# A prefix log-sum-exp: running sums moved from fp16 matmuls into VectorE adds and 18 fp32 matmuls a tile

## Chip, cores, metric

One core of a Trainium2 chip. The metric is the device time of one execution in microseconds (us). Executions whose profile shows no disturbance are called fast.

## The reference

For an input of 4 x 4096 x 4128 fp32 (batch, row, column), every output row is the log of the sum of the exponentials of all rows up to it, column by column:

```python
def reference(x):                      # x: (4, 4096, 4128) float32
    out[:, 0, :] = x[:, 0, :]
    for t in range(1, S):
        mx = np.maximum(out[:, t-1, :], x[:, t, :])
        out[:, t, :] = mx + np.log(np.exp(out[:, t-1, :] - mx) + np.exp(x[:, t, :] - mx))
```

So it is Exp, a running sum down the rows, Ln, with 270 MB in and 270 MB out.

## The kernel before

A tile has 128 partitions with R = 3 consecutive rows each (384 rows, 6.3 MB; one tile a batch has R = 2), 44 tiles in all. A tile is worked on in four chunks of 1024 columns; the last has 32 columns more, the "tail". ScalarE writes Exp as fp16 over the tile. TensorE forms all running sums in PSUM with matrices of ones and zeros: `incl` and `excl` sum over partitions, `ident` adds a partition's next row, `pick` adds the carry of the tile above. ScalarE takes Ln out of PSUM row by row. The carry is kept by VectorE as a high and a low fp16 half.

```python
# ... (Chunk, cut)
    def head(self):
        pt = self.pt = pmain.tile([P, CH], FP32, name="pt")
        for j in range(t.r):
            for s in range(0, CH, MM):
                mm(pt[:, s:s + MM], excl if j else incl, self.e(j, s, s + MM), start=j == 0)
        if not t.first:
            for s in range(0, CH, MM):
                mm(pt[:, s:s + MM], pick, carry[self.c][:, s:s + MM])
        # ... tail cut
    def stage(self, j):
        nc.scalar.activation(t.xt[:, j, c * CH:(c + 1) * CH], pt, ACT.Ln)
        if j + 1 < t.r:
            for s in range(0, CH, MM):
                mm(pt[:, s:s + MM], ident, self.e(j + 1, s, s + MM), stop=j + 2 == t.r)
            # ... tail cut
        else:
            keep(carry[c], pt)         # VectorE: high half, then low half

# order: the Exp of chunk g + 2 is issued behind the Ln of chunks g, g - 1, g - 2
for g in range(len(chunks) + R - 1):
    for d in range(R - 1, -1, -1):
        ...
            k.stage(d)
            if k.c == last and d + 1 == k.t.r:
                k.t.store()            # then the load three tiles ahead
    if g + 2 < len(chunks):
        chunks[g + 2].exp()
    if g + 1 < len(chunks):
        chunks[g + 1].head()
```

Four tile buffers lie in SBUF; loads and stores go out on one queue, each tile one transfer in and one out.

The softmax here doesn't subtract the row's maximum and nothing guards it: scores larger than these inputs give would overflow.

Of the kernel before, what the change touches and what calls it, by code (L numbers as in the profile page):

```python
# [6 lines left out]

FP32 = mybir.dt.float32
FP16 = mybir.dt.float16
ACT = mybir.ActivationFunctionType  # L10
P = 128
R = 3
CH = 1024
MM = 512
HI, LO = 96, 32


def _constants(nc, pool):


    def tri(base, name):
        t = pool.tile([P, P], FP16, name=name)
        nc.gpsimd.memset(t, 1.0)

        nc.gpsimd.affine_select(  # L25
            out=t, in_=t, pattern=[[1, P]], compare_op=mybir.AluOpType.is_ge,
            fill=0.0, base=base, channel_multiplier=-1,
        )
        return t

    def ones_where_zero(bases, step, name):
        t = pool.tile([P, P], FP16, name=name)
        nc.gpsimd.memset(t, 0.0)
        for base in bases:
            nc.gpsimd.affine_select(  # L35
                out=t, in_=t, pattern=[[step, P]], compare_op=mybir.AluOpType.not_equal,
                fill=1.0, base=base, channel_multiplier=1,
            )
        return t

    return (
        tri(0, "incl"),
        tri(-1, "excl"),
        ones_where_zero([0], -1, "ident"),
        ones_where_zero([-(HI + 31), -(LO + 31)], 0, "pick"),
    )


@with_exitstack
def kernel(  # L50
    ctx: ExitStack,
    tc: tile.TileContext,
    x: bass.AP,
    out: bass.AP,
):






    nc = tc.nc
    B, S, D = x.shape
    assert S % P == 0
    n_main = D // CH
    tail = D - n_main * CH
    t0 = n_main * CH
    last = n_main - 1

    nc.scalar.preload_act_table_set("natural_log_exp_and_others")  # L70
    consts = ctx.enter_context(tc.tile_pool(name="consts", bufs=1))
    incl, excl, ident, pick = _constants(nc, consts)

    bufs = 4
    xpool = ctx.enter_context(tc.tile_pool(name="xpool", bufs=bufs))
    cpool = ctx.enter_context(tc.tile_pool(name="cpool", bufs=1))
    pmain = ctx.enter_context(tc.tile_pool(name="pmain", bufs=3, space=bass.MemoryType.PSUM))
    ptail = ctx.enter_context(tc.tile_pool(name="ptail", bufs=2, space=bass.MemoryType.PSUM))

    carry = [cpool.tile([P, CH], FP16, name=f"carry{c}") for c in range(n_main)]  # L80
    carry_t = cpool.tile([P, tail], FP16, name="carry_t")
    for t in (*carry, carry_t):
        nc.vector.memset(t, 0.0)  # L83

    ctx.enter_context(tc.manual_schedule())

    def mm(pt, w, rhs, start=False, stop=False):
        nc.tensor.matmul(pt, lhsT=w, rhs=rhs, start=start, stop=stop, skip_group_check=True)  # L88

    def keep(cr, pt):  # L90

        nc.vector.tensor_copy(cr[HI:HI + 32, :], pt[HI:HI + 32])  # L92
        nc.vector.tensor_tensor(  # L93
            out=cr[LO:LO + 32, :], in0=pt[HI:HI + 32], in1=cr[HI:HI + 32, :],
            op=mybir.AluOpType.subtract,
        )

    class Step:


        def __init__(self, b, row, r):
            self.b, self.row, self.r = b, row, r
            self.first = row == 0

        def dram(self, t):
            rows = t[self.b, self.row:self.row + P * self.r, :]
            return rows.rearrange("(p j) d -> p j d", j=self.r)

        def load(self):
            full = xpool.tile([P, R, D], FP32, name="xt")  # L110
            self.xt = full[:, :self.r, :]
            self.half = self.xt.bitcast(FP16)
            nc.sync.dma_start(out=self.xt, in_=self.dram(x))  # L113

        def store(self):
            nc.sync.dma_start(out=self.dram(out), in_=self.xt)  # L116

    class Chunk:
        def __init__(self, step, c):
            self.t, self.c = step, c  # L120
            self.w = D - last * CH if c == last else CH

        def e(self, j, a, b):
            return self.t.half[:, j, 2 * self.c * CH + a:2 * self.c * CH + b]

        def exp(self):
            c0, w = self.c * CH, self.w
            nc.scalar.activation(  # L128
                self.t.half[:, :, 2 * c0:2 * c0 + w], self.t.xt[:, :, c0:c0 + w], ACT.Exp,
            )  # L130

        def head(self):
            t = self.t
            pt = self.pt = pmain.tile([P, CH], FP32, name="pt")
            for j in range(t.r):
                for s in range(0, CH, MM):
                    mm(pt[:, s:s + MM], excl if j else incl, self.e(j, s, s + MM), start=j == 0)
            if not t.first:
                for s in range(0, CH, MM):
                    mm(pt[:, s:s + MM], pick, carry[self.c][:, s:s + MM])  # L140
            if self.c == last:
                self.tail_head()

        def tail_head(self):


            t, r = self.t, self.t.r
            full = ptail.tile([P, R, tail], FP32, name="qt")
            qt = self.qt = full[:, :r, :]
            to = lambda v, n: v.unsqueeze(1).to_broadcast([P, n, tail])  # L150
            for i in range(r):
                e = self.e(i, CH, CH + tail)
                mm(qt[:, i:, :], incl, to(e, r - i), start=i == 0)
                if i:
                    mm(qt[:, :i, :], excl, to(e, i))
            if not t.first:
                mm(qt, pick, to(carry_t, r))

        def stage(self, j):

            t, c, pt = self.t, self.c, self.pt
            nc.scalar.activation(t.xt[:, j, c * CH:(c + 1) * CH], pt, ACT.Ln)  # L162
            if j + 1 < t.r:
                for s in range(0, CH, MM):
                    mm(pt[:, s:s + MM], ident, self.e(j + 1, s, s + MM), stop=j + 2 == t.r)
                if c == last and j == 0:
                    nc.scalar.activation(t.xt[:, :, t0:D], self.qt, ACT.Ln)  # L167
                    keep(carry_t, self.qt[:, t.r - 1, :])
            else:
                keep(carry[c], pt)  # L170

    steps = []
    for b in range(B):
        n = S // P
        parts = [R] * (n // R) + ([n % R] if n % R else [])
        if b == 0:
            parts.reverse()
        row = 0
        for r in parts:
            steps.append(Step(b, row, r))  # L180
            row += P * r
        assert row == S

    chunks = [Chunk(s, c) for s in steps for c in range(n_main)]
    ahead = bufs - 1
    for s in steps[:ahead]:
        s.load()
    stored = 0
    chunks[0].exp()
    chunks[1].exp()  # L190
    chunks[0].head()
    for g in range(len(chunks) + R - 1):
        for d in range(R - 1, -1, -1):
            if 0 <= g - d < len(chunks) and d < chunks[g - d].t.r:
                k = chunks[g - d]
                k.stage(d)
                if k.c == last and d + 1 == k.t.r:
                    k.t.store()
                    if stored + ahead < len(steps):
                        steps[stored + ahead].load()  # L200
                    stored += 1
        if g + 2 < len(chunks):
            chunks[g + 2].exp()
        if g + 1 < len(chunks):
            chunks[g + 1].head()


# [28 lines left out]
```

## Time and profile before

| | before |
|---|---|
| time, median of 3 runs (lowest to highest) | 1262.96 us (1262.78 to 1263.07) |
| bytes moved, mean rate | 541 MB, 429 GB/s |
| ScalarE, TensorE, VectorE busy | 75%, 55%, 36% |
| mean granted TensorE clock | 0.77 |

The lines that carry the argument stand in the prediction. In its busy rows each digit is the busy share of a fortieth of the span in tenths; a group line gives the code line, engine, operation and shapes, the count, then busy us and mean ns of one, then the idle time before it and what ended it; a line of waits gives the total us, the number of waits and the longest one; a line of a timeline gives start and length in us, and `x3` merges three instructions in a row. A line of a table by stretches gives the busy us of each engine, then the granted clock, the DMA share and GB/s.

### The profile page before, as it was taken

The page shows a single profiled execution, that of the slowest core. Times are in us where ns is not written, and L with a number is a line of the kernel's source. Part 1 is how long each engine was busy: PE and PEld are TensorE (multiplying, and loading weights), DVE is VectorE, ACT ScalarE, POOL GpSimd, SP SyncE. Part 2 cuts the span into 40 slices and gives each one's busy share as a digit, 9 for nine tenths or more (in the row PEclk, how much of TensorE's full clock was granted, in tenths as well). Part 3 has the DMA queues.
Part 4 walks back from the last instruction along what each step waited for, and adds up shares of the span by engine and source line. Part 5 has one row for each costly group of instructions (what it writes and reads, how often), then busy time and mean ns, then how long its engine had stood idle before and what let it go on. Part 6 is the DMA issues. An engine that isn't in the chain of part 4 may idle for free.

```text
span 1261.0 us, 6165 instructions
## 1 busy us (share of the span) xinstructions
PE 688.7 (55%) x2268; PEld 237.0 (19%) x2268; DVE 451.4 (36%) x445; ACT 947.3 (75%) x733; POOL 2.2 (0%) x13
## 2 busy tenths in 40 slices
PE   3665554555555555655346555555634755664552
PEld 1222111111121111211112211111211211221120
DVE  2443333333333333334424333333442433333344
ACT  5997777777777777778569777777966977777794
POOL 0000000000000000000000000000000000000000
PEclk9887777777677777777768777787777777778786
DMA  9999999999999999999999999999999999999998
GB/s 411 410 439 431 432 427 434 438 430 432 433 437 431 432 432 436 432 427 436 431 433 436 437 429 431 436 436 432 430 434 435 432 431 432 434 435 431 433 422 347
DMA packets 12702, 541.46 MB, mean 429 GB/s; under 512 B 1408, under 2 KB 1408, under 8 KB 1408
## 3 DMA queue, kind: packets, MB, share of 16 engines
q1 hardware_dynamic: 12672, 541.07, 99.4%
q8 instruction: 18, 0.29, 0.1%
q14 instruction: 12, 0.10, 0.0%
HBM read 270.53 MB, written 270.53 MB: 429 GB/s over the span
## 4 chain that ended last, share of the span: by engine, by line
DMA 69%; ACT 21%; PE 5%; issue 2%; DVE 1%; SPq 0%; ACTq 0%
DMA xt<-in_x_dram 67%; ACT xt L128 11%; ACT xt L162 10%; PE pt L88 5%; DMA out_dram<-xt 2%; ACT xt L167 0%; SPq L116 0%; DVE carry L92 0%; DVE carry L93 0%; ACTq L231 0%; SPq L113 0%; ACTq L128 0%; PE qt L88 0%
## 5 line engine op out<-in xcount | busy, mean ns | idle before, releaser
L128 ACT ACTIVATE xt<-xt 128x3072 f16<-128x3072 f32 (+3 forms) x176 | 478.5, 2719 | 247.9 <-DMA xt<-in_x_dram 247.8
L88 PE MATMUL pt<-xt,ident 128*128 128x512 f16 x672 | 251.3, 470 | 530.7 <-ACT xt L162 530.4
L162 ACT ACTIVATE xt<-pt 128x1024 f32<-128x1024 f32 x512 | 487.6, 1030 | 2.5 <-PE pt L88 0.7
L92 DVE CAST carry<-pt 32x1024 f16<-32x1024 f32 x176 | 216.4, 1230 | 761.0 <-ACT xt L162 760.7
L88 PE MATMUL pt<-xt,excl 128*128 128x512 f16 x672 | 247.0, 504 | 0.0
L93 DVE TENSOR_TENSOR carry<-pt,carry 32x1024 f16<-32x1024 f32 x176 | 215.9, 1227 | 6.1
L88 PEld LDWEIGHTS <-ident 128*128 128x128 f16 x672 | 70.1, 104 | 677.7 <-issue 654.0
L88 PE MATMUL pt<-xt,incl 128*128 128x512 f16 x352 | 152.0, 526 | 23.6 <-ACT xt L128 15.0
L88 PEld LDWEIGHTS <-excl 128*128 128x128 f16 x756 | 92.5, 124 | 141.0 <-issue 108.1
L88 PE MATMUL pt<-carry,pick 128*128 128x512 f16 x320 | 109.8, 429 | 0.0
L88 PEld LDWEIGHTS <-incl 128*128 128x128 f16 x480 | 45.2, 111 | 129.7 <-DVE carry L93 95.2
L88 PEld LDWEIGHTS <-pick 128*128 128x128 f16 x360 | 40.6, 113 | 57.0 <-issue 34.3
L167 ACT ACTIVATE xt<-qt 128x96 f32<-128x96 f32 (+1 forms) x44 | 10.9, 249 | 45.7 <-PE pt L88 45.7
L92 DVE CAST carry_t<-qt 32x32 f16<-32x32 f32 x44 | 8.7, 197 | 25.5 <-ACT xt L167 25.4
L88 PE MATMUL qt<-xt,incl 128*128 128x64 f16 (+2 forms) x128 | 12.3, 196 | 0.0
L88 PE MATMUL qt<-xt,excl 128*128 128x64 f16 (+1 forms) x84 | 10.6, 187 | 0.0
L93 DVE TENSOR_TENSOR carry_t<-qt,carry_t 32x32 f16<-32x32 f32 x44 | 8.5, 193 | 1.5
L88 PE MATMUL qt<-carry_t,pick 128*128 128x96 f16 (+1 forms) x40 | 8.2, 204 | 0.0
L83 DVE MEMSET carry<- 128x512 uint32 x4 | 1.9, 485 | 1.1 <-PEq L220 1.0
L70 ACT ACT_TABLE_LOAD x1 | 1.3, 1283 | 0.8 <-PEq L220 0.8
L35 POOL TENSOR_SCALAR_AFFINE_SELECT pick<-pick 128x128 f16<-128x128 f16 x2 | 0.6, 294 | 0.1
L25 POOL TENSOR_SCALAR_AFFINE_SELECT incl<-incl 128x128 f16<-128x128 f16 x1 | 0.3, 294 | 0.0
(11 smaller groups left out, 1.9 us busy)
## 6 DMA issues: line engine op xcount, KB each, us to landing
xt<-in_x_dram SPq DMA_DIRECT2D x40, 6192.0 KB, 42.2
out_dram<-xt SPq DMA_DIRECT2D x40, 6192.0 KB, 28.1
xt<-in_x_dram SPq DMA_DIRECT2D x4, 4128.0 KB, 37.3
out_dram<-xt SPq DMA_DIRECT2D x4, 4128.0 KB, 23.0
```

The lines of the kernel that those rows point to most:

```text
L25: nc.gpsimd.affine_select(out=t, in_=t, pattern=[[1, P]], compare_op=mybir.AluOpType.is_ge, fill=0.0, base=base, channel_multiplier=-1,)
L35: nc.gpsimd.affine_select(out=t, in_=t, pattern=[[step, P]], compare_op=mybir.AluOpType.not_equal, fill=1.0, base=base, channel_multiplier=1,)
L70: nc.scalar.preload_act_table_set("natural_log_exp_and_others")
L83: nc.vector.memset(t, 0.0)
L88: nc.tensor.matmul(pt, lhsT=w, rhs=rhs, start=start, stop=stop, skip_group_check=True)
L92: nc.vector.tensor_copy(cr[HI:HI + 32, :], pt[HI:HI + 32])
L93: nc.vector.tensor_tensor(out=cr[LO:LO + 32, :], in0=pt[HI:HI + 32], in1=cr[HI:HI + 32, :], op=mybir.AluOpType.subtract,)
L128: nc.scalar.activation(self.t.half[:, :, 2 * c0:2 * c0 + w], self.t.xt[:, :, c0:c0 + w], ACT.Exp,)
L162: nc.scalar.activation(t.xt[:, j, c * CH:(c + 1) * CH], pt, ACT.Ln)
L167: nc.scalar.activation(t.xt[:, :, t0:D], self.qt, ACT.Ln)
```

## The change

The intent: fp32 throughout, no halves, and far fewer instructions. Exp stays fp32 in place. VectorE adds a partition's rows to one another (`own`); one `excl` matmul on the partition's last row adds the partitions above into a PSUM tile `above` that lives through the whole kernel; VectorE adds `above` to all rows at once (`add_above`); a `pick` matmul then starts the next tile's `above` from the last row. One Ln a chunk, in place.

```diff
-    carry = [cpool.tile([P, CH], FP16, name=f"carry{c}") for c in range(n_main)]
+    above = [psum.tile([P, CH], FP32, name=f"above{c}") for c in range(n_main)]
 ...
+        def act(self, func):
+            v = self.t.xt[:, :, self.a:self.b]
+            nc.scalar.activation(v, v, func)
+        def own(self):
+            for j in range(1, self.t.r):
+                v = x[:, j, self.a:self.b]
+                add(v, x[:, j - 1, self.a:self.b], v)
         def head(self):
-            for j in range(t.r): ... incl, excl
+            for s in range(0, CH, MM):
+                mm(above[self.c][:, s:s + MM], excl, t.xt[:, t.r - 1, a + s:a + s + MM],
+                   start=t.first, stop=True)
+        def add_above(self):
+            v = t.xt[:, :, a:a + CH]
+            add(v, v, above[self.c].unsqueeze(1).to_broadcast([P, t.r, CH]))
+        def pick(self, s0=0, s1=CH):
+            if not t.final:
+                for s in range(s0, s1, MM):
+                    mm(above[self.c][:, s:s + MM], pick, t.xt[:, t.r - 1, a + s:a + s + MM],
+                       start=True)
 ... (the tail: two small matmuls, one add and one copy; cut)
+    for g, k in enumerate(chunks):
+        if g + 1 < len(chunks):
+            chunks[g + 1].own()
+            chunks[g + 1].head()
+        if g + 2 < len(chunks):
+            chunks[g + 2].act(ACT.Exp)
+        if g:
+            finish(chunks[g - 1])      # tail add, pick of the last 512 columns
+            result(chunks[g - 1])      # Ln; behind the last chunk: store, load three ahead
+        k.add_above()
+        if k.c == last:
+            k.tail_head()
+            k.pick(0, CH - MM)
+        else:
+            k.pick()
```

More of the change, by code (lines that the diff above doesn't have):

```diff
@@ L8 @@
 FP32 = mybir.dt.float32
-FP16 = mybir.dt.float16
 ACT = mybir.ActivationFunctionType
@@ L14 @@
 MM = 512
-HI, LO = 96, 32
 def _constants(nc, pool):
-    def tri(base, name):
-        t = pool.tile([P, P], FP16, name=name)
-        nc.gpsimd.memset(t, 1.0)
-        nc.gpsimd.affine_select(
-            out=t, in_=t, pattern=[[1, P]], compare_op=mybir.AluOpType.is_ge,
-            fill=0.0, base=base, channel_multiplier=-1,
-        )
-        return t
-    def ones_where_zero(bases, step, name):
-        t = pool.tile([P, P], FP16, name=name)
-        nc.gpsimd.memset(t, 0.0)
-        for base in bases:
-            nc.gpsimd.affine_select(
-                out=t, in_=t, pattern=[[step, P]], compare_op=mybir.AluOpType.not_equal,
-                fill=1.0, base=base, channel_multiplier=1,
-            )
-        return t
-    return (
-        tri(0, "incl"),
-        tri(-1, "excl"),
-        ones_where_zero([0], -1, "ident"),
-        ones_where_zero([-(HI + 31), -(LO + 31)], 0, "pick"),
-    )
+    excl = pool.tile([P, P], FP32, name="excl")
+    nc.gpsimd.memset(excl, 1.0)
+    nc.gpsimd.affine_select(
+        out=excl, in_=excl, pattern=[[1, P]], compare_op=mybir.AluOpType.is_ge,
+        fill=0.0, base=-1, channel_multiplier=-1,
+    )
+    pick = pool.tile([P, P], FP32, name="pick")
+    nc.gpsimd.memset(pick, 0.0)
+    nc.gpsimd.affine_select(
+        out=pick, in_=pick, pattern=[[0, P]], compare_op=mybir.AluOpType.not_equal,
+        fill=1.0, base=-(P - 1), channel_multiplier=1,
+    )
+    return excl, pick
 @with_exitstack
@@ L71 @@
     consts = ctx.enter_context(tc.tile_pool(name="consts", bufs=1))
-    incl, excl, ident, pick = _constants(nc, consts)
+    excl, pick = _constants(nc, consts)
     bufs = 4
@@ L76 @@
     cpool = ctx.enter_context(tc.tile_pool(name="cpool", bufs=1))
-    pmain = ctx.enter_context(tc.tile_pool(name="pmain", bufs=3, space=bass.MemoryType.PSUM))
-    ptail = ctx.enter_context(tc.tile_pool(name="ptail", bufs=2, space=bass.MemoryType.PSUM))
-    carry = [cpool.tile([P, CH], FP16, name=f"carry{c}") for c in range(n_main)]
-    carry_t = cpool.tile([P, tail], FP16, name="carry_t")
-    for t in (*carry, carry_t):
-        nc.vector.memset(t, 0.0)
+    psum = ctx.enter_context(tc.tile_pool(name="psum", bufs=1, space=bass.MemoryType.PSUM))
+    above = [psum.tile([P, CH], FP32, name=f"above{c}") for c in range(n_main)]
+    above_t = above[last][:, CH - MM:CH - MM + tail]
+    carry_t = cpool.tile([P, tail], FP32, name="carry_t")
+    nc.vector.memset(carry_t, 0.0)
     ctx.enter_context(tc.manual_schedule())
@@ L88, in mm, with add @@
         nc.tensor.matmul(pt, lhsT=w, rhs=rhs, start=start, stop=stop, skip_group_check=True)
-    def keep(cr, pt):
-        nc.vector.tensor_copy(cr[HI:HI + 32, :], pt[HI:HI + 32])
-        nc.vector.tensor_tensor(
-            out=cr[LO:LO + 32, :], in0=pt[HI:HI + 32], in1=cr[HI:HI + 32, :],
-            op=mybir.AluOpType.subtract,
-        )
+    def add(o, a, b):
+        nc.vector.tensor_tensor(out=o, in0=a, in1=b, op=mybir.AluOpType.add)
     class Step:
@@ L103, in __init__ @@
             self.first = row == 0
+            self.final = row + P * r == S
         def dram(self, t):
@@ L111, in load @@
             self.xt = full[:, :self.r, :]
-            self.half = self.xt.bitcast(FP16)
             nc.sync.dma_start(out=self.xt, in_=self.dram(x))
@@ L120, in __init__ @@
             self.t, self.c = step, c
-            self.w = D - last * CH if c == last else CH
-        def e(self, j, a, b):
-            return self.t.half[:, j, 2 * self.c * CH + a:2 * self.c * CH + b]
-        def exp(self):
-            c0, w = self.c * CH, self.w
-            nc.scalar.activation(
-                self.t.half[:, :, 2 * c0:2 * c0 + w], self.t.xt[:, :, c0:c0 + w], ACT.Exp,
-            )
-        def head(self):
+            self.a, self.b = c * CH, D if c == last else (c + 1) * CH
@@ new lines, in act @@
+        def act(self, func):
+            v = self.t.xt[:, :, self.a:self.b]
+            nc.scalar.activation(v, v, func)
+        def own(self):
+            x = self.t.xt
+            for j in range(1, self.t.r):
+                v = x[:, j, self.a:self.b]
+                add(v, x[:, j - 1, self.a:self.b], v)
+        def head(self):
+            t, a = self.t, self.a
+            for s in range(0, CH, MM):
+                mm(above[self.c][:, s:s + MM], excl, t.xt[:, t.r - 1, a + s:a + s + MM],
+                   start=t.first, stop=True)
@@ L133, in head, with tail_head @@
+        def add_above(self):
+            t, a = self.t, self.a
+            v = t.xt[:, :, a:a + CH]
+            add(v, v, above[self.c].unsqueeze(1).to_broadcast([P, t.r, CH]))
+        def pick(self, s0=0, s1=CH):
+            t, a = self.t, self.a
+            if not t.final:
+                for s in range(s0, s1, MM):
+                    mm(above[self.c][:, s:s + MM], pick, t.xt[:, t.r - 1, a + s:a + s + MM],
+                       start=True)
+        def tail_head(self):
             t = self.t
-            pt = self.pt = pmain.tile([P, CH], FP32, name="pt")
@@ L135, in head @@
-            for j in range(t.r):
-                for s in range(0, CH, MM):
-                    mm(pt[:, s:s + MM], excl if j else incl, self.e(j, s, s + MM), start=j == 0)
             if not t.first:
-                for s in range(0, CH, MM):
-                    mm(pt[:, s:s + MM], pick, carry[self.c][:, s:s + MM])
-            if self.c == last:
-                self.tail_head()
-        def tail_head(self):
-            t, r = self.t, self.t.r
-            full = ptail.tile([P, R, tail], FP32, name="qt")
-            qt = self.qt = full[:, :r, :]
-            to = lambda v, n: v.unsqueeze(1).to_broadcast([P, n, tail])
-            for i in range(r):
-                e = self.e(i, CH, CH + tail)
-                mm(qt[:, i:, :], incl, to(e, r - i), start=i == 0)
-                if i:
-                    mm(qt[:, :i, :], excl, to(e, i))
-            if not t.first:
-                mm(qt, pick, to(carry_t, r))
@@ L159, in stage @@
-        def stage(self, j):
-            t, c, pt = self.t, self.c, self.pt
-            nc.scalar.activation(t.xt[:, j, c * CH:(c + 1) * CH], pt, ACT.Ln)
-            if j + 1 < t.r:
-                for s in range(0, CH, MM):
-                    mm(pt[:, s:s + MM], ident, self.e(j + 1, s, s + MM), stop=j + 2 == t.r)
-                if c == last and j == 0:
-                    nc.scalar.activation(t.xt[:, :, t0:D], self.qt, ACT.Ln)
-                    keep(carry_t, self.qt[:, t.r - 1, :])
-            else:
-                keep(carry[c], pt)
+                mm(above_t, pick, carry_t, start=True)
@@ L172, with tail_add @@
+            mm(above_t, excl, t.xt[:, t.r - 1, t0:D], start=t.first, stop=True)
+        def tail_add(self):
+            t = self.t
+            v = t.xt[:, :, t0:D]
+            add(v, v, above_t.unsqueeze(1).to_broadcast([P, t.r, tail]))
+            if not t.final:
+                nc.vector.tensor_copy(carry_t[96:, :], t.xt[96:, t.r - 1, t0:D])
     steps = []
@@ L188, with finish, result @@
     stored = 0
-    chunks[0].exp()
-    chunks[1].exp()
-    chunks[0].head()
-    for g in range(len(chunks) + R - 1):
-        for d in range(R - 1, -1, -1):
-            if 0 <= g - d < len(chunks) and d < chunks[g - d].t.r:
-                k = chunks[g - d]
-                k.stage(d)
-                if k.c == last and d + 1 == k.t.r:
-                    k.t.store()
-                    if stored + ahead < len(steps):
-                        steps[stored + ahead].load()
-                    stored += 1
-        if g + 2 < len(chunks):
-            chunks[g + 2].exp()
-        if g + 1 < len(chunks):
-            chunks[g + 1].head()
+    def finish(k):
+        if k.c == last:
+            k.tail_add()
+            k.pick(CH - MM)
+    def result(k):
+        nonlocal stored
+        k.act(ACT.Ln)
+        if k.c == last:
+            k.t.store()
+            if stored + ahead < len(steps):
+                steps[stored + ahead].load()
+            stored += 1
+    chunks[0].act(ACT.Exp)
+    chunks[1].act(ACT.Exp)
+    chunks[0].own()
+    chunks[0].head()
+    for g, k in enumerate(chunks):
+        if g + 1 < len(chunks):
+            chunks[g + 1].own()
+            chunks[g + 1].head()
+        if g + 2 < len(chunks):
+            chunks[g + 2].act(ACT.Exp)
[3 more added lines that the diff above has]
+        k.add_above()
+        if k.c == last:
+            k.tail_head()
+            k.pick(0, CH - MM)
+        else:
+            k.pick()
+    finish(chunks[-1])
+    result(chunks[-1])
 _INS = ['x']
```

## The prediction

> **What bounds the kernel now.** I read the page from the top: busy shares, the DMA rows, the queue, and the chain.
>
> ```profile
> PE 688.7 (55%) x2268; PEld 237.0 (19%) x2268; DVE 451.4 (36%) x445; ACT 947.3 (75%) x733; POOL 2.2 (0%) x13
> DMA  9999999999999999999999999999999999999998
> q1 hardware_dynamic: 12672, 541.07, 99.4%
> DMA 69%; ACT 21%; PE 5%; issue 2%; DVE 1%; SPq 0%; ACTq 0%
> xt<-in_x_dram SPq DMA_DIRECT2D x40, 6192.0 KB, 42.2
> out_dram<-xt SPq DMA_DIRECT2D x40, 6192.0 KB, 28.1
> ```
>
> No compute engine is above 75%; the transfers fill every slice but the last. The diff leaves them as they are: x in once, out once, 541 MB. The 42.2 us of a load and 28.1 us of a store are mostly queueing: 6192 KB (6.34 MB) at the 433 GB/s of the middle slices is 14.6 us, so a load waits behind about two such transfers and a store behind one. Next, who waits for whom, and one period of ScalarE and of the issuing queue in the middle:
>
> ```profile
> ACT xt L128 <- DMA xt<-in_x_dram: 247.8, 42, 12.2
> SPq L116 <- ACT xt L162: 1178.4, 44, 30.0
> ```
> ```profile
> 539.25 2.76 ACT L128 ACTIVATE xt<-xt 128x3072 f16<-128x3072 f32 x1 [6.04 <-DMA xt<-in_x_dram]
> ...
> 568.50 2.76 ACT L128 ACTIVATE xt<-xt 128x3072 f16<-128x3072 f32 x1 [5.99 <-DMA xt<-in_x_dram]
> ```
> ```profile
> 584.34 0.34 SPq L116 DMA_DIRECT2D out_dram<-xt  x1
> 584.78 0.38 SPq L113 DMA_DIRECT2D xt<-in_x_dram  x1
> ```
>
> ScalarE, the busiest engine, stands still for a load in every step. A full step takes 568.50 - 539.25 = 29.25 us, two transfers of 14.6 us. When a load lands (568.50) the queue still holds the store and the load issued a step earlier, 29.2 us of work. The next pair is issued 15.8 us later (584.34), so **13 us of slack** is left before the DMA would run dry. So the question is not what the engines' sums are, but whether a step still fits 29.25 us and whether its store still comes less than 29 us after the next load's landing. Slack is missing only at the ends:
>
> ```profile
> 37.00 0.35 SPq L116 DMA_DIRECT2D out_dram<-xt  x1
> ```
> ```profile
> 1225.00:1230.00 5.00, 2.21 (x9) 0.69 (x8) 2.41 (x4) 4.32 (x6) 0.00 (x0) 1.00 0.76 327
> 1230.00:1235.00 5.00, 3.98 (x10) 1.28 (x10) 2.88 (x4) 5.00 (x5) 0.00 (x0) 0.66 0.48 201
> 1235.00:1240.00 5.00, 2.75 (x12) 1.02 (x12) 4.87 (x5) 4.29 (x5) 0.00 (x0) 1.00 0.78 337
> ```
>
> The first store goes out at 37.0; the three opening loads (16.9 MB, from about 2 us) end near 41, so today it comes in time. Between 1225 and 1240 the DMA share falls to 0.48: the last load is in and the second-last store is not yet issued.
>
> **The durations I price with.**
>
> ```profile
> L128 ACT ACTIVATE xt<-xt 128x3072 f16<-128x3072 f32 x120 | 332.1, 2767 | 233.1 <-DMA xt<-in_x_dram 233.1
> L162 ACT ACTIVATE xt<-pt 128x1024 f32<-128x1024 f32 x512 | 487.6, 1030 | 2.5 <-PE pt L88 0.7 <-PE qt L88 0.3
> L93 DVE TENSOR_TENSOR carry<-pt,carry 32x1024 f16<-32x1024 f32 x176 | 215.9, 1227 | 6.1
> ```
> ```profile
> 38.80 1.03 PE L88 MATMUL pt<-xt,excl 128*128 128x512 f16 x4
> 39.66 0.59 PE L88 MATMUL pt<-carry,pick 128*128 128x512 f16 x2
> ...
> 664.20 1.93 PE L88 MATMUL pt<-xt,ident 128*128 128x512 f16 x4 [2.44 <-ACT xt L162]
> 665.92 1.06 PE L88 MATMUL pt<-xt,incl 128*128 128x512 f16 x2
> ```
>
> Start to start, a 512-column fp16 matmul takes (39.66 - 38.80)/4 = 0.215 us where the clock is granted and (665.92 - 664.20)/4 = 0.43 us where it is not.
>
> **What the Trainium skill says.** "VectorE: DVE Perf Modes", on the TRN2 errata, gives an fp32 tensor_tensor add (N+151)/0.96 ns, that is 1224 ns for N = 1024; the subtract above measured 1227 ns, with PSUM as source. It agrees, though on 32 partitions. "TensorE: Matmul & The Clock Gate", Part 1, gives N/1.2 ns cold and N/2.4 + 2.5 ns warm: 427 and 216 ns, which the two spacings confirm. "FP8 and Floating Point Precision", TensorE Precision Notes, says that true fp32 takes four passes through the array; no run so far has an fp32 matmul, so this price is the least certain. "DMA: Bandwidth & Descriptors", Specifications, puts the fabric's ceiling at 435 GB/s; the page shows 429 over the span, so there is nothing to win on transfers.
>
> **The change, part by part, for a full step** (three row groups, four chunks; 40 such steps, and 4 with two row groups).
>
> *ScalarE.* Exp stays, in place in fp32: 4 x about 2.77 us. The 12 Ln of 1030 ns and one of 250 ns become 4 Ln of Exp's shape, 2.77 us, and successive ones overlap by 0.1. 8 x 2.67 + 0.2 for the wider chunk's two = 21.6 us, where it now takes 3 x 2.76 + 2.89 + 12 x 0.9 + 0.15 = 22.1. No change worth counting; busy stays near 950 us (75%).
>
> *VectorE.* The 8 carry copies and subtracts on 32 partitions go (9.8 us). In come six 1024-wide adds at 1.23 (7.4), two of 1056 at 1.26 (2.5), four 3072-wide at (3072+151)/0.96 = 3.36 us (13.4), and the tail's add and copy (0.26 + 0.20). Sum **23.8 us of 29.25**, 81%. With two row groups it is 3 x 1.23 + 1.26 + 4 x 2.29 + 0.4 = 14.5. In all 40 x 23.8 + 4 x 14.5 = 1010 us, 80%: VectorE becomes the busiest engine.
>
> *TensorE.* Some 52 fp16 matmuls become 16 of 512 columns and 2 of 32. Four passes make 4 x 0.215 = 0.86 us warm, 1.71 cold: 13.8 us or 27.3 us a step, plus under 1 us for the small ones. Even wholly cold it stays below 29.25, and a TensorE that busy should get its clock. I expect 60 to 75% busy.
>
> *Waits.* In a steady step, t = 0 at the load's landing: ScalarE does Exp, Ln (old chunk 1), Exp, Ln (2), Exp, Ln (3), then the store of the old tile goes out. VectorE: the first own sum at 2.8 to 5.2, the add for old chunk 3 to 8.6, the second own sum (its Exp is in at 8.1) to 11.1, the old tile's tail add to 11.4. ScalarE reaches the last Ln at 5 x 2.67 = 13.4, so the tail add is in time and the store goes out at **16.2 us against 15.8 now**. VectorE goes on: add to 14.8, own 17.2, add 20.6, own 23.2, add 26.6, before the next landing at 29.25. The head matmuls of a chunk run behind the 3.4 us add of the one before. Slack stays about 13 us; the middle of the kernel doesn't move.
>
> *Ends.* Start: the first store now waits for all four Ln of tile 0, three of which stand behind Exps of tile 1. That tile's first Exp starts at 27.7; from there three Exps (2.7) and three two-row Ln (1.85) give 27.7 + 8.0 + 5.6 = 41.3 us, in place of 37.0. Its first packets follow about 1.5 us after issue (an estimate from the first load: issued 0.8, moving at 2), near 42.8, while the loads end near 41: **+1.7 us** of empty DMA, never won back. End: after the last landing, three 1.8 us Exps and three 2.75 us Ln give the second-last store at 13.7 us in place of 12.9 (1220.8 to about 1233.6): **+0.8 us**. The last store comes about 25 us after the landing, still before the one ahead of it has drained (about 30), so it hides.
>
> Sum: 1262.96 + 1.7 + 0.8 = **1265.4 us**.
>
> **Rivals.** *VectorE becomes the bound.* It needs over 29.25 us a step, 23% above my sum. For it: adds with two SBUF inputs on 128 partitions are not in this trace, and 80% is high. Against: the formula met the one measured add within 0.3%. If an add cost 2 cycles an element, a step would be near 46 us and the kernel 2000 us. *TensorE becomes the bound*, through four weight loads per fp32 matmul that don't hide, at 0.10 to 0.15 us each: cold, 16 x (1.71 + 0.5) = 35 us, about 1520 us in all; warm 21 us, and nothing. Against: a TensorE that never idles should be granted its clock. *The DMA slows beside heavier SBUF traffic.* 1% would be 12 us. Against: its rate is 434 GB/s both in busy and in idle stretches of the engines. *A gain*: the DMA floor, 541 MB at 434 GB/s, is 1247 us, so 2% faster (1238) is out of reach.
>
> **Range and chances.** Transfers alone bound it from below, and the ends' terms are each good to a microsecond: 1262 to 1270 holds it 8 times in 10. Faster by over 2%: 0.01. Within 2%: 0.94. Slower: 0.05, nearly all from the TensorE and VectorE rivals.
>
> **What would show it.** Right: the queue at 99% of the span, first store near 41, steady steps of 29.2 us with stores about 16 us after a landing, ScalarE still waiting for loads, VectorE near 1010 us with 3.36 us adds, 512-column fp32 matmuls 0.86 or 1.71 us apart. Wrong: DMA digits under 9 in the middle, ScalarE waiting for VectorE or TensorE in place of loads, 3072-wide adds far over 3.4 us, fp32 matmuls over 1.8 us, or stores over 29 us after a landing.

## The result, and the profile after

| | before | changed |
|---|---|---|
| time, median of 4 runs | 1262.97 us | 1264.09 us (1263.63 to 1268.05) |
| the same on another chip | 1262.83 us (9 runs) | 1265.39 us (1265.19 to 1265.54, 5 runs) |
| VectorE busy | 451 us (36%) | 981 us (77%) |
| TensorE busy, granted clock | 689 us (55%), 0.77 | 761 us (60%), 0.87 |

The ratio of the two is 1.0016 (95% interval 0.9996 to 1.0036) in the first set and 1.002 (1.0007 to 1.0032) in the second. Ratios are the mean time of one kernel's fast runs over that of the other's of the same rounds, so not quite the ratio of the medians. By the second set the change costs a fifth of a per cent. The profiled run of the first set happened to be its longest, 1268.05 us; the one on the other chip was 1265.3. I read timelines from the first and sums from both.

The page of the changed kernel: busy shares, the DMA row, the queue and the chain.

```profile
PE 760.5 (60%) x1512; PEld 289.0 (23%) x1512; DVE 980.6 (77%) x597; ACT 923.8 (73%) x353; POOL 1.1 (0%) x8
DMA  9999999999999999999999999999999999999998
q1 hardware_dynamic: 12672, 541.07, 99.3%
DMA 67%; DVE 12%; ACT 9%; PE 8%; issue 1%; SPq 0%; ACTq 0%
```

VectorE's work has more than doubled, and the DMA row is what it was, digit for digit. The chain is still two thirds transfers. ScalarE's waits, and one full step of ScalarE and of the issuing queue in the middle:

```profile
ACT xt L106 <- DMA xt<-in_x_dram: 290.5, 42, 12.5
ACT xt L106 <- PE above L74: 33.9, 38, 4.2
```
```profile
544.47 13.38 ACT L106 ACTIVATE xt<-xt 128x3072 f32<-128x3072 f32 x5 [7.08 <-DMA xt<-in_x_dram]
558.46 8.23 ACT L106 ACTIVATE xt<-xt 128x3168 f32<-128x3168 f32 x3 [0.61 <-PE above L74]
573.72 13.38 ACT L106 ACTIVATE xt<-xt 128x3072 f32<-128x3072 f32 x5 [7.03 <-DMA xt<-in_x_dram]
```
```profile
590.57 0.34 SPq L97 DMA_DIRECT2D out_dram<-xt  x1
```

From landing to landing it is 573.72 - 544.47 = 29.25 us, the step of the kernel before to the hundredth, and ScalarE waits 7 us in each for a load. The store goes out at 590.57 - 573.72 = 16.85 us after the landing; before it was 15.84. The middle line shows why it is later than ScalarE alone would make it: ahead of a tile's last Ln ScalarE waits 0.6 us for TensorE. That Ln works in place, and a `pick` matmul is still reading the last row of the chunk.

The durations of the new work, by shape, and TensorE's pace, first in its granted clock, then in the first group behind a pause of 6.5 us:

```profile
L106 ACT ACTIVATE xt<-xt 128x3072 f32<-128x3072 f32 x240 | 645.9, 2750 | 273.0 <-DMA xt<-in_x_dram 273.0
L77 DVE TENSOR_TENSOR xt<-xt,above 128x3072 f32<-128x3072 f32 x160 | 535.7, 3348 | 1.2
L77 DVE TENSOR_TENSOR xt<-xt 128x1024 f32<-128x1024 f32 x252 | 308.1, 1222 | 248.3 <-ACT xt L106 244.0
```
```profile
26.11 1.88 PE L74 MATMUL above<-xt,pick 128*128 128x512 f32 x4
27.83 1.88 PE L74 MATMUL above<-xt,excl 128*128 128x512 f32 x4
...
579.10 3.75 PE L74 MATMUL above<-xt,excl 128*128 128x512 f32 x4 [6.51 <-DVE xt L77]
582.64 0.47 PE L74 MATMUL above<-carry_t,pick 128*128 128x32 f32 x2
```

Each fp32 matmul of the kernel leaves two matmul records, so the `x4` are two of them: (27.83 - 26.11)/2 = 0.86 us each, and (582.64 - 579.10)/2 = 1.77 us in the slow clock.

The ends: the first two stores, and the stretch behind the last load.

```profile
42.64 0.35 SPq L97 DMA_DIRECT2D out_dram<-xt  x1
...
68.38 0.34 SPq L97 DMA_DIRECT2D out_dram<-xt  x1
```
```profile
1230.00:1235.00 5.00, 4.00 (x13) 1.78 (x12) 4.46 (x5) 5.00 (x3) 0.00 (x0) 1.00 0.83 357
1235.00:1240.00 5.00, 3.50 (x9) 1.16 (x7) 5.00 (x3) 5.00 (x4) 0.00 (x0) 1.00 0.21 89
```

The first store went out at 37.0 before and goes out at 42.6 now. The table below sums, from the records of all DMA packets, the time in which the 16 engines had no packet under way (an average over the 16, in us), leaving out the first 2 us and what follows the last store's bulk. Its last column adds what packets took beyond their usual time (1.829 us for 49.5 KB, 1.222 us for 33 KB).

```
profiled run         empty, 41-46   empty, 66-72   empty, ends of batches   gap near the end   slow packets
before                   0               0                 0                     4.0               4.5
changed                  1.9             0.2               0.3                   4.9               7.7
changed, 2nd chip        2.0             0.4               0                     3.6               6.3
```

The same records show where the time is lost. Set against the kernel before by the bytes moved so far (my sum over all packets of both traces), the changed kernel on the second chip is 0.9 us behind at 44 us, 1.7 at 60, 2.7 at 90 and 4.1 at 100; from 110 to 1225 us it stays 3.3 to 4.5 behind without a trend, and its span ends 2.5 us behind. So the loss is made in the first 100 us, the middle adds nothing and the end gives some of it back. At 44 us it is 0.9 and not 1.9 us because the last opening packets of the kernel before were slow: its loads ended at 42.5 to 43.2 us, those of the changed kernel at 41.3 to 42.1.

### The profile page after: what moved, and what is told of

Read it like the earlier page. It is cut to its first block, busy times and chain, and to the rows that moved or that the text cites. A ratio compares the mean times of both kernels' runs of the same rounds, so it can differ in the third digit from the quotient of the medians.

```text
span 1266.3 us, 4623 instructions
## 1 busy us (share of the span) xinstructions
PE 760.5 (60%) x1512; PEld 289.0 (23%) x1512; DVE 980.6 (77%) x597; ACT 923.8 (73%) x353; POOL 1.1 (0%) x8
## 4 chain that ended last, share of the span: by engine, by line
DMA 67%; DVE 12%; ACT 9%; PE 8%; issue 1%; SPq 0%; ACTq 0%
DMA xt<-in_x_dram 63%; DVE xt L77 12%; ACT xt L106 9%; PE above L74 8%; DMA out_dram<-xt 5%; SPq L97 0%; ACTq L106 0%; SPq L94 0%; DVE carry_t L146 0%
## 5 line engine op out<-in xcount | busy, mean ns | idle before, releaser
L106 ACT ACTIVATE xt<-xt 128x3072 f32<-128x3072 f32 (+2 forms) x352 | 922.5, 2693 | 327.0 <-DMA xt<-in_x_dram 290.5
L74 PE MATMUL above<-xt,excl 128*128 128x512 f32 (+1 forms) x792 | 443.1, 687 | 348.7 <-DVE xt L77 339.4
L77 DVE TENSOR_TENSOR xt<-xt 128x1024 f32<-128x1024 f32 (+1 forms) x336 | 413.4, 1230 | 255.0 <-ACT xt L106 249.4
L77 DVE TENSOR_TENSOR xt<-xt,above 128x3072 f32<-128x3072 f32 (+3 forms) x220 | 582.9, 2651 | 11.7 <-PE above L74 10.3
L74 PE MATMUL above<-xt,pick 128*128 128x512 f32 x640 | 330.7, 630 | 130.0 <-DVE xt L77 130.0
L74 PEld LDWEIGHTS above<-xt,excl 128*128 128x128 f32 x792 | 162.6, 229 | 601.5 <-issue 490.5
L74 PEld LDWEIGHTS above<-xt,pick 128*128 128x128 f32 x640 | 113.6, 198 | 307.4 <-DVE xt L77 227.2
L74 PEld LDWEIGHTS above<-carry_t,pick 128*128 128x128 f32 x80 | 20.8, 271 | 51.4 <-DVE xt L77 48.2
L74 PE MATMUL above<-carry_t,pick 128*128 128x32 f32 x80 | 17.5, 308 | 10.1 <-DVE xt L77 10.1
L146 DVE COPY carry_t<-xt 32x32 f32<-32x32 f32 x40 | 7.1, 178 | 1.4
```

The costliest lines, as they stand in the source:

```text
L74: nc.tensor.matmul(pt, lhsT=w, rhs=rhs, start=start, stop=stop, skip_group_check=True)
L77: nc.vector.tensor_tensor(out=o, in0=a, in1=b, op=mybir.AluOpType.add)
L106: nc.scalar.activation(v, v, func)
L146: nc.vector.tensor_copy(carry_t[96:, :], t.xt[96:, t.r - 1, t0:D])
```

## The experiments

All were started from the changed kernel unless said otherwise. In the first four, the same chip served all.

**1. The changed kernel again.** No edit.

> The changed kernel as it is, on the chip that the three reordered ones use. The theory (transfers bound it, the reordered ends add 1.9 us of empty DMA at the first store and 0.8 us at the last): 1264 to 1266 us, 1 to 3 us over the kernel before. The rival (the 1 us seen is chance in the packets' times): the two within 0.5 us, either way round.

Measured: 1265.39 us against 1262.83 before, ratio 1.002 (1.0007 to 1.0032). The difference of 2.6 us is real and of the predicted size. In the trace, 2.4 us of empty DMA at the start are new, and the packets ran 1.8 us slower, most of it in the first 100 us; the gap near the end was 0.4 us shorter than before, not longer. That is 3.8 us, and the two spans differ by 2.5: most of the rest is idle time that the kernel before has more of, 0.6 us behind its last store, where one of the 16 engines finished after the others, and 0.3 scattered over the middle.

**2. The first tile finished early.** At the boundary behind the first tile, the Ln of a chunk go ahead of the next tile's Exp, and the tile's last add and Ln ahead of the next tile's own sums.

```diff
+    early = {n_main}
     for g, k in enumerate(chunks):
+        ends = g + 1 in early
-        if g + 1 < len(chunks):
+        if g + 1 < len(chunks) and not ends:
             chunks[g + 1].own()
             chunks[g + 1].head()
+        if (ends or g + 2 in early) and g:
+            result(chunks[g - 1])
         ... Exp of chunk g + 2; the usual finish and result unless done; add_above, pick
+        if ends:
+            finish(k)
+            result(k)
+            chunks[g + 1].own()
+            chunks[g + 1].head()
```

> At the boundary of the first tile alone, its last Ln are put ahead of the next tile's Exps. The theory: the first store goes out near 38 us in place of 42.6, before the opening loads end at 41, so the 1.9 us of empty DMA at 41 to 44 us go and the time falls by about 1.9 us against the changed kernel. The rival (compute in the middle sets the time, the start is made up later): no change against the changed kernel, within 0.5 us.

Measured: 1265.96 us (1265.28 to 1267.48), so nothing was won: the expectation failed. The queue's first two stores say why, first in this run, then in run 4, which finishes every tile early:

```profile
38.91 0.35 SPq L97 DMA_DIRECT2D out_dram<-xt  x1
...
68.61 0.34 SPq L97 DMA_DIRECT2D out_dram<-xt  x1
```
```profile
38.88 0.35 SPq L97 DMA_DIRECT2D out_dram<-xt  x1
...
64.43 0.34 SPq L97 DMA_DIRECT2D out_dram<-xt  x1
```

The first store moved to 38.9 as meant and the hole at 41 us closed. But the second store stayed at 68.6. The DMA, now 2 us ahead, ran dry before it: 3.1 us of empty DMA between 66 and 70 in place of 2.0 and 0.4. VectorE was busy 4.9 of the 5 us from 60 to 65: the first tiles are a ramp that compute sets. A hole closed at one store opens at the next. The second store did not merely stay: in run 1 a slow TensorE clock held it up (see run 3), and where the clock was granted it left at 66.6, so the early first tile itself made it some 2 us later.

**3. The last boundary alone.** The same edit with `early = {len(chunks) - n_main}`.

> At the boundary of the last tile alone, the tile before is finished ahead of the last tile's own sums. The theory: the second-last store goes out about 10 us after the last load's landing in place of 13.7, while the DMA still has a store to drain (14.6 us), so the gap of 4.9 us of empty DMA near the end shrinks below 1 us and the time falls by 4 us or more against the changed kernel, below the kernel before, near 1260. The rival (the last tile's compute sets the end, not the DMA gap): the end moves by under 1 us.

Measured: 1263.69 us (1263.35 to 1266.07), 1.7 us under the changed kernel where 4 were expected. The gap shrank as expected in kind, from 3.6 to 1.4 us, though not below 1. But the 16 engines then ended apart, twelve by 1258.0 and the last at 1260.5, where in run 1 all had ended within 0.2 us. Gap and tail together, the engines' idle time from 1223 us to the last packet, are 3.6 us here and 3.7 in run 1: in these traces the edit won nothing at the end.

In the traces, what this run won lies at the start, where the edit changes nothing: its second store left at 66.6 us and not at 68.5, and from 110 to 900 us it is some 2 us ahead of run 1 by bytes moved. The stretch from 60 to 65 us, run 1 first, shows one reason, the granted clock (the third number from the end):

```profile
60.00:65.00 5.00, 4.08 (x7) 1.74 (x7) 4.93 (x5) 1.34 (x1) 0.00 (x0) 0.66 0.73 317
60.00:65.00 5.00, 3.30 (x7) 1.35 (x8) 4.93 (x5) 2.45 (x2) 0.00 (x0) 1.00 0.73 317
```

ScalarE waited 4.25 us for matmuls there in run 1, and 2.55 us in this run. So it is not shown that the edit won the 1.7 us.

**4. Every boundary.** `early = set(range(n_main, len(chunks), n_main))`.

> The same order at every tile boundary. The theory: both ends are won, 6 us against the changed kernel, near 1258; in the middle the stores go out near 11 us after a landing in place of 16.9 and that is worth nothing, as the DMA never ran dry there. The rival (a later own sum of the next tile makes VectorE's period longer than a step): DMA digits under 9 in the middle and a time over 1270.

Measured: 1262.07 us (1262.01 to 1263.1), 3.3 us under the changed kernel where 6 were expected, and ratio 0.9996 (0.9983 to 1.0008) to the kernel before: as fast as it. No hole is left at the start, 1.6 us near the end, but stragglers ended 3.1 us behind the bulk (1259.3 against 1256.2). So what it won lies at the start: by bytes moved it is 0.5 us behind the kernel before in the mean from 110 to 600 us, where run 1 is 4.1 behind. A part of that can be the granted clock at 60 to 65 us, which was 1.00 here too. The stores in the middle go out 10.8 us after a landing and the DMA is no fuller for it.

**5. Loads taken away, kernel before.** Later tiles work on what lies in the four buffers; the output is wrong. In both one-way kernels Ln has a scale of 1/4096 to keep the numbers small.

```diff
         def load(self):
-            full = xpool.tile([P, R, D], FP32, name="xt")
-            nc.sync.dma_start(out=self.xt, in_=self.dram(x))
+            # ... (slot = self.nth % bufs; the load's own lines shortened)
+            if self.nth < bufs:        # the first four tiles only
+                tiles[slot] = xpool.tile([P, R, D], FP32, name="xt")
+                nc.sync.dma_start(...)
+            self.xt = tiles[slot][:, :self.r, :]
```

> The kernel before with a load for the first four tiles only (later steps work on the tiles that lie in the buffers, so the output is wrong on purpose; Ln gets a scale that keeps the numbers small), all stores kept: half the traffic, 14.6 us a step. The theory (transfers bound it): the time falls to what ScalarE needs, its 947 us and its 46 us of waits for TensorE, plus about 30 us at the ends, 1000 to 1050 us. The rival (compute sets the step of 29.2 us): no more than 2% below 1263.

Measured: 1016.73 us (one run, state unknown), within the expectation.

**6. Loads taken away, changed kernel.** The same edit.

> The changed kernel with the same loads taken away, wrong on purpose. The theory: VectorE's 23.8 us a step and 14.5 us for a short one show, 1010 us plus about 30 to 50 us at the ends, 1040 to 1080 us, and VectorE above 90% busy: slower in compute than the kernel before, which the transfers hide. Rivals: TensorE's fp32 matmuls with their waits set the step, over 1150 us; or compute was the bound all along, no more than 2% below 1264.

Measured: 1057.08 us (one run, state unknown), within the expectation. The busy rows of the two, before first:

```profile
PE 630.1 (62%) x2268; PEld 221.0 (22%) x2268; DVE 451.5 (44%) x445; ACT 943.1 (93%) x733; POOL 2.2 (0%) x13
```
```profile
PE 725.7 (69%) x1512; PEld 270.3 (26%) x1512; DVE 977.2 (93%) x597; ACT 919.7 (87%) x353; POOL 1.1 (0%) x8
```

With half the traffic the kernel before is bound by ScalarE (93%) and the changed one by VectorE (93%), and the changed one is 40 us slower in compute (one execution each). Both lie more than 200 us below the time under the full traffic, where the two differ by 2.6 us.

**7. One more VectorE instruction a tile.** The maximum of the first chunk with itself, 3.35 us, which changes no value.

```diff
             add(v, v, above[self.c].unsqueeze(1).to_broadcast([P, t.r, CH]))
+            if self.c == 0:
+                for _ in range(1):
+                    nc.vector.tensor_tensor(out=v, in0=v, in1=v, op=mybir.AluOpType.max)
```

> The changed kernel with one more 3072-wide VectorE instruction a step (the maximum of a chunk with itself, result unchanged): VectorE 27.2 us a step, under the 29.25 us of the transfers. The theory: the time stays within 3 us of the changed kernel. The rival (VectorE is as good as the bound): 40 steps x 3.35 us, up to 130 us more.

Measured: 1275.8 us (1273.5 to 1277.67), ratio 1.0107 (1.009 to 1.0124) to before: 10 us over the changed kernel. Both expectations failed, the 3 us by much and the 130 us by far more. The trace pointed at the ends. Near the end the DMA stood still for 7.5 us in place of 3.6 (a table by stretches; the second last number is the DMA share):

```profile
1240.00:1245.00 5.00, 2.14 (x5) 0.60 (x4) 4.93 (x4) 2.95 (x3) 0.00 (x0) 1.00 0.02 10
```

and the two holes at the start came to 4.7 us in place of 2.4. Runs 9 and 10 test that.

**8. Three of them.** `range(3)`.

> Three such instructions a step: VectorE 33.9 us a step against 29.25. The theory: the step turns over to VectorE and grows by some 4.6 us in the 40 long steps, and the 4 short ones give no more than 21.4 us: 1430 to 1470 us, with ScalarE waiting for VectorE. If VectorE had no part in the bound at all, no change; if it were the bound already, 40 x 10 = 400 us more.

Measured: 1457.88 us (one run, state unknown), as expected. The busy row, and ScalarE's largest wait:

```profile
PE 790.3 (54%) x1512; PEld 302.3 (21%) x1512; DVE 1405.7 (97%) x729; ACT 925.5 (64%) x353; POOL 1.1 (0%) x8
```
```profile
ACT xt L106 <- PE above L74: 483.2, 83, 12.9
```

VectorE is busy 97% and ScalarE's waits for loads have gone, but for the opening one (11.2 us); ScalarE's wait is put down to TensorE, whose matmuls themselves wait for VectorE. So the bound does turn over where VectorE's step exceeds the transfers', as the sums say.

**9. The extra instruction in the 38 middle tiles only.** The condition becomes `self.c == 0 and 3 <= self.t.nth < 41`.

> The extra VectorE instruction in the 38 tiles of the middle alone, none in the first three and the last three. The theory (the 10 us that it cost everywhere were lost at the two ends, where the DMA ran dry at 41 to 45, 69 to 72 and 1237 to 1246 us): within 1.5 us of the changed kernel, some 1264 to 1267 us, though VectorE does 127 us more work. The rival (each step of the middle pays a little): about 1274.

Measured: 1267.29 us (1266.46 to 1268.03), ratio 1.0035 (1.002 to 1.0049). The extra VectorE work, 125 us by the trace (36 instructions of 3.36 us and 2 of 2.29), cost 1.9 us against run 1 (other chips, the kernel before within 0.1 us on both). That misses the stated 1.5 by a little and is far from 1274. In the trace the middle pays in one place: 0.5 us of empty DMA lie at 591 us, where a batch ends with its short tile, and packets were slower by 1.6 us from 600 to 630 us; by bytes moved the run loses some 2 us from 590 to 650, and from 110 to 1225 us little more than half a us elsewhere. Packets slower by 1.0 us, from 900 to 960, stand in the first trace of the changed kernel too.

**10. In the first three and last three tiles only.** The condition negated.

> The same instruction in the first three and the last three tiles alone, 20 us of VectorE work. The theory: nearly all of the 10 us, 1272 to 1278. The rival (the middle pays): within 2 us of the changed kernel, 1267.

Measured: 1274.37 us (1271.34 to 1275.25), ratio 1.0093 (1.0076 to 1.011). Six tiles, 18 us of work by the trace (4 instructions of 3.36 us and 2 of 2.29), cost 9.0 us. So the ends pay nearly all of the 10 us, and the middle little.

**11. Every 512-column pick matmul twice.**

```diff
-                for s in range(s0, s1, MM):
+                for s in [*range(s0, s1, MM)] * 2:
                     mm(above[self.c][:, s:s + MM], pick,
```

> Every 512-column pick matmul twice (it starts its sum afresh, so the result is the same): 8 more fp32 matmuls a step at 0.86 us, TensorE some 21 us a step where its clock is granted, 29 to 35 us where it is not. The theory (TensorE has room and gets its clock): the middle stays, the last Ln of a tile waits about 0.9 us longer for the pick that reads its tile, and the ends pay 1 to 3 us: 1265 to 1269. The rival (TensorE, with its matmuls in the cold clock, is near the bound): a step over 29.25 us, 1300 us and more.

Measured: 1273.59 us (1272.41 to 1274.48), ratio 1.0084 (1.0069 to 1.0099). Neither side met it: 8.2 us over the changed kernel, not 1 to 3, and nowhere near 1300. The step did not grow to what the rival says, with TensorE at 79% and a granted clock of 0.89. Much of the loss is again at the ends, 4.9 us of empty DMA at the first store and 6.7 near the end. But the middle lost some 3.5 us as well: by bytes moved the run is 5.7 us behind the kernel before in the mean from 110 to 600 us and 9.3 from 1000 to 1225, with 0.8 us of empty DMA at 908 to 910. ScalarE, whose Ln works in place, waits longer for the picks, 88.7 us in place of 33.9:

```profile
ACT xt L106 <- PE above L74: 88.7, 48, 5.8
```

**12. Every boundary early, and the last two tiles stored in two halves of columns.**

```diff
         def store(self, a=0, b=D):
-            nc.sync.dma_start(out=self.dram(out), in_=self.xt)
+            nc.sync.dma_start(out=self.dram(out)[:, :, a:b], in_=self.xt[:, :, a:b])
 ...
+        halves = k.t.nth >= len(steps) - 2
+        if halves and k.c == 1:
+            k.t.store(0, 2 * CH)
         if k.c == last:
-            k.t.store()
+            k.t.store(2 * CH if halves else 0)
 ... (and the edit of run 4)
```

> The early order at every boundary, and the last two tiles stored in two halves of columns, the first as soon as its two chunks are done. The theory: the 1.6 us of empty DMA that the early order leaves near 1228 to 1231 us go, 1260 to 1262 us. The rival (smaller packets or one engine that finishes late eat it): 1262 or more.

Measured: 1262.5 us (1262.45 to 1262.7), ratio 0.9997 (0.9982 to 1.0012): the rival's side. The gap near 1230 is gone, and the end shows what took its place:

```profile
1250.00:1255.00 5.00, 0.00 (x0) 0.00 (x0) 0.00 (x0) 0.00 (x0) 0.00 (x0) 0.50 0.83 347
1255.00:1260.00 5.00, 0.00 (x0) 0.00 (x0) 0.00 (x0) 0.00 (x0) 0.00 (x0) 0.50 0.19 80
```

From 1252.6 us on, one engine after another runs out of work, and the last ends at 1259.3. A reading: the 16 have equal shares, the slowest sets the end, and the gap near the end had let it catch up, so closing the gap wins only part of its length. No run tests it alone, and the records do not name the engine, but the completion records, one for each engine and transfer, bear it out. Within one transfer of run 1 they lie 0.8 us apart or less for the first three, 5.0 us apart at 1218 us, and 0.2 us apart behind the gap of 3.6 us. Behind the gaps of 1.4 and 1.6 us of runs 3 and 4 they still lie 2.6 and 3.5 us apart, and 6.7 us in this run without a gap. Gap and tail together come to 4.9 us in the kernel before, 4.9 and 3.7 in the two traces of the changed one, and 3.6, 4.6 and 4.1 in runs 3, 4 and 12: closing the gap moved most of its idle time behind the last store. No version that I ran beats the kernel before by more than its interval.

## Why the prediction was right, point by point

- **The bound.** Right and shown. The middle step is 29.25 us in both kernels, ScalarE still waits for loads (290 us in place of 248), and runs 5 and 6 show compute at 1017 and 1057 us under it.
- **ScalarE's price.** Right: the one-piece Exp and Ln took 2.75 us; its busy time fell from 947 to 924 us, where I had said about 950.
- **VectorE's price.** Right within 3%: adds of 3348 and 1222 ns against 3.36 and 1.23 us, a total of 981 us against 1010. Independent adds overlap by some 0.09 us: a 3.35 us add at 532.49 ended at 535.84 and the next had begun at 535.75.
- **TensorE's price.** Right: 0.86 us warm as predicted, 1.77 cold against 1.71, 60% busy, at the low edge of 60 to 75.
- **Waits in the middle.** The store was predicted 16.2 us after a landing and came at 16.85. Missed: the in-place Ln of the last chunk waits for the `pick` that reads its row. In the middle it costs nothing.
- **The start, +1.7 us.** The hole had the size (1.9 and 2.0 us, with 0.2 to 0.4 at the second store), but by errors that offset each other: the first store came at 42.6, not 41.3, by that same missed wait (1.2 us here), the opening loads ended near 41.7, not 41, and the store's first packets moved 0.9 us after its issue, not 1.5. And the cause given, the Ln behind the next tile's Exps, is only part of it: run 2 took it away and the hole moved to the second store. The whole start cost more than the hole, some 4 us by bytes moved after 100 us. The clock had a part: it was 0.66 from 60 to 65 us in both traces, where the prediction took TensorE to have room.
- **The end, +0.8 us.** The store came as predicted, 13.6 us after the landing against 12.9 before. That it costs 0.8 us is not confirmed: the gap was 4.9 us against 4.0 in the first trace and 3.6 in the second, and gap and tail together 4.9 and 3.7 against 4.9.
- **The sum.** That 1.7 + 0.8 met the measured 2.6 us is in part luck. In the second trace the start cost some 4 us and the end gave back 1.4, so one term was too small and the other had the wrong sign. Slower packets, 1.8 us in that trace, are part of the start's loss; why they are slower in the first 100 us stays open.
- **Rivals.** VectorE as the bound needs more than 3.35 us more a step (run 7) and less than 10 (run 8); by the sums it is 29.25 - 23.8 = 5.45. TensorE with half as many large matmuls again kept its clock (0.89, run 11). A slower DMA in the middle under heavier traffic is not seen: 29.25 us a step, and in the second trace no trend from 110 to 1225 us.
- **Slack.** I had called it 13 us in the middle and "missing only at the ends", and said too little of that: 18 us of VectorE work in the six end tiles cost 9 us (run 10), as several stores in a row arrive late at each end.

## What to carry to other kernels

In a kernel that transfers bound, price a change by two questions: does a step of the new busiest engine still fit the transfers' step, and when does each store at the two ends go out against the moment the queue runs dry. Here the middle forgave nearly everything up to that step (125 us of work for 1.9 us), and the first tiles almost nothing. At the end, by these traces, a gap of up to some 4 us cost nothing of its own, since the DMA engines had drifted 5 to 7 us apart; a longer one did cost (7.6 us in the trace of run 10). An operation in place waits for all other readers of its data, matmuls included (0.6 us a step here). Compare traces stretch by stretch before giving a gain to an edit: run 3 gained where nothing had been edited. And closing one hole in the DMA pays only if the next store is in time as well.

## What the Trainium skill lacked or had wrong

- "FP8 and Floating Point Precision", TensorE Precision Notes, gives the four passes and no time. Measured: 0.86 us for a 512-column fp32 matmul in a stream, 1.77 us in the slow clock, two matmul and two weight-load records each; it is 4 x 0.215, so the weight loads were hidden.
- "VectorE: DVE Perf Modes", TRN2 errata, reports its formula for fp32 adds as exact at N of 512 and 2048; it lacks a PSUM operand broadcast over three rows. The formula held for that too, at N = 3072 on 128 partitions: 3348 ns measured against 3357.
- "VectorE: DVE Perf Modes", The DRAIN you can't avoid, says that a next op that is not held starts earlier, and gives no time for it. Independent adds started about 0.09 us before the one ahead had ended, and the groups' busy times sum to 1004 us where the engine was busy 981, 2% less.
- "DMA: Bandwidth & Descriptors" has no figure for how far the 16 engines drift apart over a long stream: their last packets ended 6.7 us apart (1252.6 to 1259.3 us) where the end had no gap, and within 0.2 us where it had one of 3.6 us.
- No page has the cost of the first turn from loads alone to loads and stores: packets of 49.5 KB took 1.83 us as a rule, but up to 3.25 us (median 2.8) where they started from 38 to 40 us in the kernel before, whose first store was issued at 37.0, and 1.83 us there in the changed kernel, whose first store was not yet issued.
